# A hybrid encoder layer on one core: the sample's attention first, norms in two stages, block sums under eight fill units

## The chip, the cores and the metric

The kernel runs on one core of one Trainium2 chip. The metric is the device time of one execution in microseconds (us). The kernel before took 868.57 us (median of three executions, 867.28 to 869.51).

## What is computed

The layer treats two sequences with the same weights: a prompt of 512 tokens and a sample of 256. Together they are six blocks of 128 tokens: blocks 0 to 3 are the prompt, 4 and 5 the sample. In the reference, cut to what matters:

```
def mixer(h, ...):
    proj = h @ w_in
    cq, ckv, kr, conv_a, conv_g = jnp.split(proj, cut, axis=-1)
    q = rms_norm(cq, q_norm_g) @ w_uq        # 8 heads, 64 + 32 (rotary)
    kv = rms_norm(ckv, kv_norm_g) @ w_ukv
    ...
    attn = block_attention(qf, kf, v)        # every query sees every key of its sequence
    u = conv_a * jax.nn.sigmoid(conv_g)
    u = depthwise_conv(u, dw_w, width 31) + dw_b
    u = jax.nn.silu(layer_norm(u, conv_ln_g, conv_ln_b))
    merged = jnp.concatenate([rms_norm(attn, attn_out_g), rms_norm(u, conv_out_g)], axis=-1)
    return merged @ w_out

x = x + mixer(rms_norm(x, norm1_g), ...)
x = x + (jax.nn.silu(h @ w_gate) * (h @ w_up)) @ w_down    # h = rms_norm(x, norm2_g)
y = rms_norm(x, final_g)
```

## The kernel before

Matmul operands are split into two fp32r parts (`split`: a cast on ACT, L107 or L110, and a subtraction on DVE, L108 or L111), and a product is three matmuls, high with high, high with low and low with high. All PE matmuls of products go through one helper, `mm`, so they share line L286.

The work runs in stages.

1. Input projections (`pc`, `pq`, `pt`). While they run, the depthwise convolution begins on DVE: 31 taps for each of four channel groups of each sequence, one instruction a tap (L250, writing `acc`; 128x512 for the prompt, 128x256 for the sample). `mm` hands out taps in step with the matmuls (`tap_some`, at a `pace`), the prompt's first. `acc_112` to `acc_115` are the prompt's channel groups, `acc_116` to `acc_119` the sample's.
2. Up-projections: keys (`k_up`, `pku`), values (`v_up`, `pv`), queries (`q_up`, `pqu`, one call a block, its output scaled on ACT and rotated on DVE by `rope`).
3. Attention in twelve units. A prompt unit is one head over four blocks, a sample unit two heads over two blocks. Each unit transposes its queries (`st_q`, `ptq`), multiplies by the keys (`st_s`, `pss`), takes the row maximum on DVE (`ngmx`), the exponential on ACT, transposes the result (`st_t`, `ptp`), copies it on ACT (`PT`) and multiplies by the values (`st_v`, `po`). `unit_step(i)` issues the scores of unit i and the values of unit i-1. Before, the prompt's eight units come first, then the sample's four.
4. Between the units the convolution is finished: `conv_ln` transposes `acc` (`pcl`), takes mean and variance on DVE, an inverse root on POOL, and writes `z` on ACT; `conv_act` transposes back (`pca`), applies the swish on ACT and DVE, squares, and sums the squares on PE with a matrix of ones (`prc`); `conv_split` splits it. `attn_norm` transposes the attention output (`pan`), scales it on DVE to `z`, transposes it back (`pcb`) and splits it.
5. Output projection. `out_conv(b, o, ...)` is the convolution's half for block b and half o of the columns (`pe`, 12 matmuls 128x512), `out_attn` the attention's half (`bank<-wr`). Each ends with an addition to the residual on DVE (`xall`, L766).
6. `x1_norm` of each block: squares on ACT, inverse root on POOL, scaling (L902 on DVE, L904 on ACT), transposes (L907) and copies to `raw`.
7. Feed-forward. Gate and up products use a seven-product scheme on 2x2 blocks of the weights and of the normed input: m1 and m2 use parts B11 and B21 of the input alone, p5, p6, p7 and p4 use its block sums T1, T2, T3, T4, and p3 uses B22. `t_sums` makes the sums of one third of the columns: four DVE operations and four splits. There are 22 units f; three fill units (`NFILL = 3`) run m1 and m2 first, kept in SBUF, and the main loop `g_rest(f)` then runs five products for them and all seven for the others. A product is 12 matmuls 128x384.
8. Down products, final norm, output.

A scheduler orders each engine's queue; each engine works its queue in order. The instructions are issued by the program in the order written, but the scheduler may move an instruction ahead of others on its engine. All DMAs named here are issued on SP's queue.

Pools of SBUF are closed and reused: the attention's `qh` and `ql` lie in memory that `rope` used before, so the first cast to `qh` waits for the last of `rope`. T1 and T2 before lie where the attention's normed parts lie (`mT`), so `t_sums` can't write them until `out_attn` has read those.

## Time and profile before

| | |
|---|---|
| median of the runs | 868.57 us (867.28 to 869.51) |
| profiled execution, time | 872.94 us |
| profiled execution, span | 871.2 us |
| PE busy | 824.6 us (95%) |
| DVE busy | 718.0 us (82%) |
| ACT busy | 438.7 us (50%) |
| POOL busy | 79.0 us (9%) |
| mean granted TensorE clock | 0.975 |
| DMA moved | 108.27 MB |

Durations below come from the one profiled execution. PE and PEld overlap: a weight load runs beside the matmul before it. Two things in PE's row cost time: idle time, and time in which the granted clock is below 1.00, since the same matmuls then take longer.

### The profile page before, as it was taken

The numbers are of one execution on the slowest core, as the hardware profiler recorded it, in microseconds if no ns is written. First come the engines' busy times: TensorE is split into PE (matmuls) and PEld (weight loads), VectorE is DVE, ScalarE is ACT, GpSimd is POOL, SyncE is SP. The second block draws the span as 40 slices with busy tenths as digits, with TensorE's granted clock in tenths as the row PEclk, the third lists the DMA queues.
The fourth block names the chain that finished last, engine by engine and source line by source line (L and its number), as shares of the span: only waits on it lengthen the run. The fifth ranks groups of instructions, "written<-read, shape, count | busy, mean of one in ns | idle before, by whom it ended". The sixth has DMA issues, their size and how long they took to land.

```text
span 871.2 us, 12428 instructions
## 1 busy us (share of the span) xinstructions
PE 824.6 (95%) x4381; PEld 735.8 (84%) x4381; DVE 718.0 (82%) x1310; ACT 438.7 (50%) x886; POOL 79.0 (9%) x113
## 2 busy tenths in 40 slices
PE   5999999899998889979999999999999999999996
PEld 4888997866675667769999999999999988888785
DVE  3699989988878745799998787888898778989994
ACT  5623338777778063584343333343433445556743
POOL 1000341000101010100000000000000000003273
PEclk9999999989989969989999999999999999999999
DMA  8722102300001113224433334443434599963343
GB/s 273 277 68 85 43 1 80 140 1 1 1 1 58 40 48 123 96 72 131 145 124 103 125 103 142 139 143 123 159 125 151 165 319 335 309 216 117 110 134 144
DMA packets 46638, 108.27 MB, mean 124 GB/s; under 512 B 4720, under 2 KB 18032, under 8 KB 46576
## 3 DMA queue, kind: packets, MB, share of 16 engines
q1 hardware_dynamic: 46400, 107.09, 36.7%
q8 instruction: 34, 0.56, 0.3%
q10 hardware_dynamic: 144, 0.39, 0.1%
q14 instruction: 28, 0.23, 0.1%
q0 software_dynamic: 32, 0.00, 0.0%
HBM read 88.20 MB, written 19.27 MB: 123 GB/s over the span
## 4 chain that ended last, share of the span: by engine, by line
PE 79%; DVE 10%; ACT 3%; issue 3%; DMA 2%; POOL 1%; POOLq 0%; ACTq 0%
PE bank L286 51%; PE pc L286 7%; PE pe L286 4%; PE pss L286 3%; PE pq L286 3%; PE po L286 2%; PE pt L286 2%; DVE acc L250 2%; PE ptp L695 2%; DVE wr L108 1%; DMA st<-xT 1%; PE pku L286 1%; DVE ra L108 1%; PE prc L286 1%; DVE ra L491 1%
## 5 line engine op out<-in xcount | busy, mean ns | idle before, releaser
L286 PE MATMUL bank<-ra,wr 128*128 128x384 f32 x1056 | 188.0, 336 | 0.0
L286 PEld LDWEIGHTS bank<-ra,wr 128*128 128x128 f32 x1056 | 184.7, 187 | 0.0
L286 PE MATMUL bank<-sa,wr 128*128 128x384 f32 x792 | 145.4, 341 | 4.9 <-DVE wr L108 4.9
L286 PEld LDWEIGHTS bank<-sa,wr 128*128 128x128 f32 x792 | 141.3, 191 | 5.2 <-DVE wr L108 5.2
L286 PE MATMUL bank<-wr,wr 128*128 128x512 f32 x594 | 135.2, 389 | 1.7 <-DVE wr L108 1.7
L250 DVE SCALAR_TENSOR_TENSOR acc<-u,c,acc 128x512 f32<-128x512 f32 (+1 forms) x240 | 133.0, 608 | 0.1
L286 PEld LDWEIGHTS bank<-wr,wr 128*128 128x128 f32 x594 | 111.4, 188 | 25.2 <-DVE wr L108 2.1
L107 ACT CAST wr<-sr 128x512 fp32r<-128x512 f32 (+1 forms) x107 | 65.7, 616 | 84.4 <-PE bank L286 83.0
L107 ACT CAST wr<-vt 128x512 fp32r<-128x512 f32 x88 | 54.6, 621 | 93.3 <-PE bank L286 83.9
L108 DVE TENSOR_TENSOR wr<-sr,wr 128x512 fp32r<-128x512 f32 (+1 forms) x107 | 72.6, 681 | 18.7 <-ACT wr L107 18.6
L1112 POOL TENSOR_SCALAR fme<-fms 128x1 f32<-128x1 f32 x6 | 27.7, 4608 | 440.3 <-ACT vt L1102 440.1
L286 PE MATMUL pc<-ra,sa 128*128 128x256 f32 (+1 forms) x288 | 56.1, 357 | 9.6 <-ACT ra L110 9.6
L286 PEld LDWEIGHTS pc<-ra,sa 128*128 128x128 f32 x288 | 47.0, 200 | 17.7 <-ACT ra L110 10.5
L108 DVE TENSOR_TENSOR wr<-vt,wr 128x512 fp32r<-128x512 f32 x88 | 60.1, 685 | 0.0
L107 ACT CAST wr<-ra 128x384 fp32r<-128x384 f32 x51 | 26.1, 513 | 37.6 <-PE bank L286 21.8
L108 DVE TENSOR_TENSOR wr<-ra,wr 128x384 fp32r<-128x384 f32 x51 | 28.1, 551 | 9.7 <-ACT wr L107 8.7
L286 PE MATMUL pe<-sa,ra 128*128 128x512 f32 x120 | 32.4, 423 | 2.2 <-ACT sa L110 1.2
L286 PE MATMUL bank<-wr,ra 128*128 128x512 f32 x144 | 34.4, 395 | 0.0
L286 PE MATMUL pq<-sa,ra 128*128 128x384 f32 x108 | 33.8, 342 | 0.0
L678 ACT ACTIVATE sa<-pss,ngmx 128x512 f32<-128x512 f32 (+1 forms) x48 | 29.5, 626 | 7.2 <-DVE ngmx L675 7.2
L286 PE MATMUL pss<-ra,qh 96*128 96x512 f32 (+1 forms) x96 | 31.2, 403 | 1.6 <-ACT sa L678 0.9
L675 DVE TENSOR_REDUCE ngmx<-pss 128x1 f32<-128x512 f32 (+1 forms) x40 | 26.8, 684 | 6.3 <-PE pss L286 5.6
(219 smaller groups left out, 1340.7 us busy)
## 6 DMA issues: line engine op xcount, KB each, us to landing
sr<-wgu SPq DMA_DIRECT2D x47, 512.0 KB, 3.8
sr<-wdn SPq DMA_DIRECT2D x34, 512.0 KB, 4.4
sumd<-xall SPq DMA_DIRECT2D x44, 192.0 KB, 1.9
ra<-sumd SPq DMA_DIRECT2D x44, 192.0 KB, 5.0
actd<-xall SPq DMA_DIRECT2D x11, 384.0 KB, 2.3
xall<-actd SPq DMA_DIRECT2D x11, 384.0 KB, 2.9
st<-wconv SPq DMA_DIRECT2D x7, 512.0 KB, 6.3
xr<-xtok SPq DMA_DIRECT2D x6, 512.0 KB, 6.6
```

Of the source, the lines that this page charges most:

```text
L107: ACT.copy(dst_hi, src)
L108: DVE.tensor_sub(dst_lo, src, dst_hi.bitcast(F32))
L250: yield n / 512, lambda j=j: DVE.scalar_tensor_tensor(a, us[:, j : j + n], w(j), a, ALU.mult, ALU.add)
L286: PE.matmul(out, lhsT, rhs, start=start, stop=stop)
L491: DVE.tensor_sub(lo, src, hi.bitcast(F32))
L675: DVE.tensor_reduce(mx, ps.rearrange("p (j n) -> p j n", j=m), AX.X, ALU.max, negate=True)
L678: ACT.activation(P[:, js], ps[:, js], AF.Exp, bias=ngmx[:, b0 + b, h : h + 1], accum_out=asum[:, b0 + b, h : h + 1],)
L695: PE.transpose(pt[:, o : o + 128], P[b][:, j * n + kt * 128 : j * n + (kt + 1) * 128], ident)
L1112: POOL.tensor_scalar(fme[b], fms[:, 2 * b + 1 : 2 * b + 2], 1.0, EPS, ALU.mult, ALU.add)
```

## The change

Five things are moved or made new; nothing in the number of products changes.

- The attention units are reordered: the sample's four first, then the prompt's eight. `q_up(0)` moves ahead of the sample's `k_up`, and the others run 4, 5, 1, 2, 3. The copies of the rotated key are reordered to match. `conv_ln(0)` now stands after unit 4 (`LN0 = 4`, before 6), `attn_norm(4)` and `(5)` after unit 8, and the prompt's four `attn_norm` after the last unit.
- `attn_norm` and `conv_act` are cut into two stages (`attn_norm1` and `2`, `conv_act1` and `2`), with projection parts written between them; from there on PE's transposes and matmuls are pinned to the written order (`pinned`). The `out_conv(4, 0)` and `(5, 0)` move behind them, into the eight-bank stage.
- The attention's half (`mT`) and the convolution's half (`cvT`) get regions of their own, and T1 to T4 are laid so that T1 and T3 lie over the convolution's half.
- The blocks of the output projection and `x1_norm` run 4, 0, 1, 5, 2, 3; the transposes of `x1_norm` become `x1_turn`, written one or two blocks later.
- There are eight fill units. Their m1 and gate value are written to DRAM (`filld`) and loaded again by `g_rest`. `t_sums` makes two splits (T3, T1), and `t_split2` the other two (T2, T4); they are written behind the first fill units, block column 1 ahead of them. For f = 0, p5 and p7 run before p6. The gate weights of five more units are loaded twice.

The core of the diff:

```diff
-LN0 = 6
+LN0 = 4
...
     def mm(out, lhsT, rhs, start, stop):
-        PE.matmul(out, lhsT, rhs, start=start, stop=stop)
+        pinned(PE.matmul(out, lhsT, rhs, start=start, stop=stop))
...
     kr_up(0)
+    q_up(0)
     for p in range(4):
         k_up(p, 1)
...
-    for b in range(NB):
+    for j, b in enumerate((4, 5, 1, 2, 3)):
         q_up(b)
...
-    units = [(0, (h,)) for h in range(H)] + [(1, (2 * p, 2 * p + 1)) for p in range(H // 2)]
+    units = [(1, (2 * p, 2 * p + 1)) for p in range(H // 2)] + [(0, (h,)) for h in range(H)]
...
-    mT = rtiles()
+    mT = mtiles((0, 4096))
+    cvT = mtiles((8192, 6144))
...
         if i == LN0:
             tap_all(0)
+            pace["s"] = 1.0
+            pin[0] = True
             conv_ln(0)
             conv_ln(1)
+            pin[0] = False
...
-            attn_norm(2, mT)
-            attn_norm(3, mT)
-        elif i == LN0 + 5:
+            attn_norm(4)
+            attn_norm(5)
             conv_split(0)
+        elif i == LN0 + 7:
             wc0 = conv_w(0)
...
+    oc(0, 0)
+    oc(1, 0)
     wc1 = conv_w(1)
...
+    pin[0] = True
...
+    attn_norm1(0)
+    attn_norm1(1)
+    oc(2, 0)
+    attn_norm2(0)
+    attn_norm2(1)
+    attn_norm1(2)
+    attn_norm1(3)
+    oc(3, 0)
+    attn_norm2(2)
+    attn_norm2(3)
...
+    oc(0, 1)
     tap_all(1)
+    oc(1, 1)
     conv_ln(4)
     conv_ln(5)
-    attn_norm(4, mT)
-    attn_norm(5, mT)
-    conv_act(1)
+    oc(2, 1)
+    for k in range(4):
+        conv_act1(1, k)
+    oc(3, 1)
+    for k in range(4):
+        conv_act2(1, k)
     conv_split(1)
...
-    T1, T2, T3, T4 = [[blk(ra_, 2 * i + w) for w in range(2)] for i in range(4)]
+    T2, T4, T3, T1 = [[blk(ra_, 2 * i + w) for w in range(2)] for i in range(4)]
...
+        if f < NFILL:
+            nc.sync.dma_start(filld[f], units_g[f])
...
+        if f < NFILL:
+            A = x_pair()
+            nc.sync.dma_start(A, filld[f])
...
-    NFILL = 3
+    NFILL = 8
...
+    both(4)
+    both(0)
+    x1_turn(4)
+    both(1)
+    x1_turn(0)
+    both(5)
+    x1_turn(1)
...
+    for f in range(3):
+        gs_load(f)
+    both(2)
+    split(wx[0], wx[1], gs[0][:, KA])
+    t_sums(1)
+    out_attn(3, 0, wa[0])
+    gw[0] = wx, wpair(gs[0][:, KB])
+    x1_turn(5)
+    x1_turn(2)
+    out_attn(3, 1, wa[1])
+    prep(1)
+    x1_norm(3)
+    behind = {0: lambda: t_sums(2), 1: lambda: t_sums(0), 2: lambda: t_split2(1), 3: lambda: t_split2(2), 4: lambda: t_split2(0)}
     for f in range(NFILL):
...
+        gs_load(f + 3)
+        g_m1(f, gs[f], gw[f][0])
+        prep(f + 2)
+        if f in behind:
+            behind[f]()
+        g_m2(f, gs[f], gw[f][1])
+        if f == 0:
+            x1_turn(3)
+    pin[0] = False
```

Where this moves instructions, at the three places of which the prediction speaks. The line numbers of the changed kernel differ (`mm` is L293 there, `conv_ln`'s transposes L570, L107 and L108 are the same).

PE's queue at the start of the attention, before. `ptq` are query transposes, `pcl` the transposes of `conv_ln`, `pss` scores:

```order
L650 MATMUL ptq_1796<-ident,sa_171_1423 96x128 x4
L563 MATMUL pcl_2245<-ident,acc_112 128x128
L563 MATMUL pcl_2245<-ident,acc_113 128x128
L563 MATMUL pcl_2245<-ident,acc_114 128x128
L563 MATMUL pcl_2262<-ident,acc_112 128x128
L563 MATMUL pcl_2262<-ident,acc_113 128x128
L563 MATMUL pcl_2262<-ident,acc_114 128x128
L563 MATMUL pcl_2245<-ident,acc_115 128x128
L563 MATMUL pcl_2262<-ident,acc_115 128x128
L286 MATMUL pss_1805<-ra_69,qh_1790 128x512 x2
```

The same place on PE in the changed kernel:

```order
L686 MATMUL ptq_1798<-ident,sa_171_1423 96x128 x4
L293 MATMUL pss_1807<-ra_69,qh_1790 128x256 x2
L293 MATMUL pss_1817<-ra_69,qh_1790 128x256 x2
L293 MATMUL pss_1841<-ra_69,qh_1803 128x256 x2
L293 MATMUL pss_1807<-ra_69,ql_1791 128x256
L293 MATMUL pss_1807<-ra_69,qh_1790 128x256 x2
```

The eight `pcl` transposes of blocks 0 and 1 have moved from here to the place behind the fourth sample unit, and the first scores are a sample unit's.

PE's queue from the end of the output projection's convolution half, before: `pan` and `pcb` are the transposes of `attn_norm`, `pca` and `prc` those and the sums of `conv_act`:

```order
L563 MATMUL pcl_3011<-ident,acc_119 128x128
L611 MATMUL pan_3028<-ident,attnT_1773 128x128 x4
L621 MATMUL pcb_3036<-ident,z_3033 128x128 x4
L611 MATMUL pan_3048<-ident,attnT_1773 128x128 x4
L583 MATMUL pca_3069<-ident,z_3009 128x128
L583 MATMUL pca_3069<-ident,z_3026 128x128
L621 MATMUL pcb_3056<-ident,z_3053 128x128 x4
L583 MATMUL pca_3091<-ident,z_3009 128x128
L583 MATMUL pca_3091<-ident,z_3026 128x128
L286 MATMUL prc_3068<-ones,th_3073 128x2 x2
```

The same place on PE in the changed kernel, from the last value products (`po`) on:

```order
L293 MATMUL pe_2818<-sa_387_2738,ra_69 128x512 x11
L642 MATMUL pan_2850<-ident,attnT_1772 128x128 x4
L642 MATMUL pan_2857<-ident,attnT_1772 128x128 x4
L293 MATMUL pe_2864<-sa_387_2738,ra_69 128x512 x12
L656 MATMUL pcb_2884<-ident,z_2855 128x128 x4
L656 MATMUL pcb_2897<-ident,z_2862 128x128 x4
L642 MATMUL pan_2910<-ident,attnT_1772 128x128 x4
L642 MATMUL pan_2917<-ident,attnT_1772 128x128 x4
L293 MATMUL pe_2924<-sa_387_2738,ra_69 128x512 x12
L656 MATMUL pcb_2943<-ident,z_2915 128x128 x4
L656 MATMUL pcb_2956<-ident,z_2922 128x128 x4
L293 MATMUL pe_2969<-sa_397_2837,ra_69 128x512 x12
```

Projection parts of 12 matmuls now stand between the two transposes of a norm, and the norm is that of the prompt's blocks; `pcl` of blocks 4 and 5 comes 24 `pe` matmuls after the last `pcb`, one more part stands between it and `pca`, and one between `pca` and `prc`.

DVE's queue where the block sums are made, before: `b` are the raw blocks, `ra` the sums' parts, L920 to L926 are `t_sums`, L958 is the addition of a fill unit's m2, and `wr` are parts of the fill units' weights:

```order
L108 TENSOR_TENSOR ra_69<-b_3229,ra_69 128x4x128 x2
L922 TENSOR_TENSOR b_3229<-b_3228,b_3229 128x4x128
L926 TENSOR_TENSOR b_3229<-b_3229,b_3230 128x4x128
L958 TENSOR_TENSOR xall<-bank_3162,xall 128x384
L108 TENSOR_TENSOR ra_69<-b_3229,ra_69 128x4x128 x2
L924 SCALAR_TENSOR_TENSOR b_3229<-b_3229,b_3231 128x4x128
L108 TENSOR_TENSOR wr_3217<-sr_3225,wr_3216 128x512
L108 TENSOR_TENSOR wr_3219<-sr_3226,wr_3218 128x512
```

The same place on DVE in the changed kernel (L997 to L1002 are `t_sums`, L1039 is the addition of m2):

```order
L997 TENSOR_TENSOR vt_1418<-b_3227,b_3225 128x512
L1039 TENSOR_TENSOR xall<-bank_3128,xall 128x384
L999 TENSOR_TENSOR b_3225<-b_3224,b_3225 128x4x128
L108 TENSOR_TENSOR ra_69<-vt_1418,ra_69 128x4x128
L1001 SCALAR_TENSOR_TENSOR b_3227<-b_3225,b_3227 128x4x128
L108 TENSOR_TENSOR wr_3215<-sr_3223,wr_3214 128x512
L1002 TENSOR_TENSOR b_3226<-b_3227,b_3226 128x4x128
L108 TENSOR_TENSOR ra_69<-b_3225,ra_69 128x4x128
L108 TENSOR_TENSOR wr_3217<-sr_3223,wr_3216 128x512
```

The splits of the fill units' weights (`wr`), which stood behind most of the block sums, now stand between them, and 16 products wait for no sum where six did.

More of the change, by code (lines that the diff above doesn't have):

```diff
@@ L573, in conv_ln, with conv_act1 @@
         cz[b] = z
-    def conv_act(s):
+    prcs = {}
+    def conv_act1(s, i):
         b0, nb = SB[s]
         n = SEQ[s][1]
-        pr = pst("o" if s == 0 else "s", "prc")
-        for i in range(4):
-            pt = pst("l", "pca")
-            for b in range(nb):
-                PE.transpose(pt[:, b * 128 : (b + 1) * 128], cz[b0 + b][:, i * 128 : (i + 1) * 128], ident)
+        pt = pst("l", "pca")
+        for b in range(nb):
+            pinned(PE.transpose(pt[:, b * 128 : (b + 1) * 128], cz[b0 + b][:, i * 128 : (i + 1) * 128], ident))
+        if s == 0:
@@ L591, in conv_act @@
-            ACT.activation(th[:, :n], d, AF.Square, scale=0.5 * CC ** -0.5)
-            for b in range(nb):
-                mm(
-                    pr[:, 2 * b : 2 * b + 2], th[:, b * 128 : (b + 1) * 128], ones[:, :2],
-                    start=(i == 0 and b == 0), stop=(i == 3 and b == nb - 1),
-                )
+        else:
+            h = slice(i % 2 * 256, i % 2 * 256 + 256)
+            if i == 0:
+                prcs["y"] = tmp.tile([128, 512], F32, tag="th", name=nm("yt"), bufs=3)
+            if i % 2 == 0:
+                prcs["h"] = tmp.tile([128, 512], F32, tag="th", name=nm("th"), bufs=3)
+            yt, th = prcs["y"][:, h], prcs["h"][:, h]
@@ new lines, in conv_act1, with conv_act2 @@
+        g, bb = c[:, C_LG + i : C_LG + i + 1], c[:, C_LB + i : C_LB + i + 1]
+        ACT.activation(yt[:, :n], pt[:, :n], AF.Identity, bias=bb, scale=g)
+        ACT.activation(th[:, :n], yt[:, :n], AF.Tanh, scale=0.5)
+        d = acc_cols(s, i)
+        DVE.scalar_tensor_tensor(d, th[:, :n], 1.0, yt[:, :n], ALU.add, ALU.mult)
+        ACT.activation(th[:, :n], d, AF.Square, scale=0.5 * CC ** -0.5)
+        prcs[s, i] = th
+    def conv_act2(s, i):
+        b0, nb = SB[s]
+        if i == 0:
+            prcs[s] = pst("o", "prc")
+        pr, th = prcs[s], prcs.pop((s, i))
+        for b in range(nb):
+            mm(
+                pr[:, 2 * b : 2 * b + 2], th[:, b * 128 : (b + 1) * 128], ones[:, :2],
+                start=(i == 0 and b == 0), stop=(i == 3 and b == nb - 1),
+            )
+        if i < 3:
+            return
@@ L769, in w, with oc @@
         def w(k):
[L770 to L772 removed]
+            return [t[:, (k % 2) * 512 : (k % 2 + 1) * 512] for t in wc_[k // 2]]
+        out_mm(p, b, cvT, w)
         out_add(p, b, o, rc)
+    def oc(b, o):
+        out_conv(b, o, wc1 if o else wc0, pst("s", "pe"))
     st_q(0)
@@ L1013, in tile_hybrid_layer, with both @@
     wa = [attn_w(o) for o in range(2)]
-    for b in range(3):
+    wx = [wxp.tile([128, 512], F32R, name=f"wx{i}") for i in range(2)]
+    def both(b):
         for o in range(2):
```

159 lines of the change are left out of this document (86 added, 73 removed).

## The prediction

> **What bounds the kernel now.** I read the page first, then the busy time by stage, then PE's waits, then the queues of DVE and ACT where PE waits. The page says that PE is the bound on average:
>
> ```profile
> PE 824.6 (95%) x4381; PEld 735.8 (84%) x4381; DVE 718.0 (82%) x1310; ACT 438.7 (50%) x886; POOL 79.0 (9%) x113
> ```
>
> So only PE's idle time and its time at a lower clock can be won. By stage (the columns are the stretch, its length, then busy time with instructions of PE, PEld, DVE, ACT and POOL, then the granted clock):
>
> ```profile
> 137.00:176.25 39.25, 32.84 (x191) 30.03 (x189) 38.77 (x78) 30.96 (x68) 0.00 (x0) 0.99 0.24 93
> 176.25:279.50 103.25, 97.86 (x537) 68.40 (x537) 85.71 (x176) 78.51 (x192) 9.51 (x22) 0.92 0.01 3
> 279.50:323.70 44.20, 37.35 (x162) 30.27 (x161) 27.09 (x56) 16.33 (x35) 4.54 (x12) 0.85 0.16 55
> 323.70:396.90 73.20, 63.91 (x306) 54.24 (x305) 55.66 (x89) 41.15 (x84) 5.71 (x12) 0.95 0.30 101
> 396.90:820.00 423.10, 423.10 (x2272) 403.21 (x2272) 362.91 (x649) 187.30 (x343) 9.18 (x3) 1.00 0.50 168
> ```
>
> These are: end of the up-projections; attention; projection of the convolution's half with the last norms; projection of the attention's half, block sums, fill units and the first block-sum product; the rest. Loss is idle time plus busy time times one less the clock: 6.4 in the first; 5.4 + 0.08 x 97.9 = 13.2 in the second; 6.9 + 0.15 x 37.4 = 12.5 in the third; 9.3 + 0.05 x 63.9 = 12.5 in the fourth; none in the fifth. Together 44.6 us, the most that could be won; the change leaves the start and the end alone. PE's waits between 137 and 400 us (total, times, longest):
>
> ```profile
> PE bank L286 <- DVE wr L108: 4.9, 1, 4.9
> PE pan L611 <- ACT z L572: 3.6, 1, 3.6
> PE bank L907 <- DVE vt L902: 3.2, 5, 0.7
> PE pcl L563 <- DVE acc L250: 2.9, 1, 2.9
> PE po L286 <- ACT PT L697: 2.3, 1, 2.3
> PE pku L286 <- DVE ck L108: 1.7, 1, 1.7
> ```
>
> Five of these six names are places that the change rewrites; the reader is to ask of each what ends last there once it is gone.
>
> **First stretch, 137 to 176 us: nothing.** Moving `q_up(0)` ahead of the sample's `k_up` gives PE 18 matmuls to run while DVE makes `ck`, so the wait of 1.7 goes. Moving `pcl` away takes the wait of 2.9 out. But DVE was busy 38.77 of the 39.25 us, and ACT's first cast to `qh` shows who ends last:
>
> ```profile
> 175.62 1.07 ACT L107 CAST qh<-ptq 96x512 fp32r<-96x512 f32 x2 [5.18 <-DVE sa L371]
> ```
>
> It waits 5.18 us for the last `rope`, which stands at the end of DVE's backlog (the same 120 prompt taps and 5 sample taps, splits and ropes in both kernels). PE comes there earlier and waits longer; scores start at about 176.3 as before. The price: the eight `pcl` transposes that ran in this shadow must run later, in PE's busy time.
>
> **Second stretch, attention.** Where its loss of 13.2 lies, with that of later places:
>
> ```profile
> 176.25:186.00 9.75, 9.75 (x35) 7.68 (x36) 7.16 (x13) 5.57 (x15) 0.00 (x0) 0.69 0.00 0
> 250.00:265.00 15.00, 13.88 (x76) 11.97 (x76) 8.22 (x16) 8.95 (x25) 3.08 (x6) 0.66 0.00 1
> 265.00:280.00 15.00, 11.29 (x73) 7.52 (x74) 14.87 (x31) 14.93 (x40) 1.74 (x4) 1.00 0.09 26
> 300.00:305.00 5.00, 1.08 (x8) 0.60 (x6) 2.02 (x6) 1.55 (x2) 1.98 (x6) 1.00 0.00 0
> 305.00:315.00 10.00, 8.08 (x29) 6.30 (x30) 3.60 (x7) 6.03 (x15) 1.49 (x4) 0.51 0.16 52
> 383.00:395.00 12.00, 7.31 (x26) 7.31 (x27) 11.22 (x20) 7.21 (x12) 0.00 (x0) 0.72 0.37 105
> ```
>
> The start costs 0.31 x 9.75 = 3.0 in clock, after the idle time before it. 250 to 265 costs 1.1 + 0.34 x 13.9 = 5.8: short sample units mixed with `prc` and transposes. 265 to 280 costs 3.7, with ACT busy 14.93 of 15: exponentials, casts of `conv_split`, squares and `conv_w` at once. The change puts the short units where nothing else is to be done, and the convolution's work among the prompt's long units, where the stretch as a whole has ACT busy 78.5 of 103. So the 5.8 and 3.7 should shrink. Not to nothing: `conv_ln` now takes four groups of transposes through two banks in two units, each through a chain of 4.5 us (below), and the sample units at the start are short chains at a half clock. The trace doesn't show that mix. The loss besides the start was 10.2; bounds are 0 and 12 (a fifth more, if the chains wait); I take 6, just past the middle, since ACT stays the nearest limit. Rates of PE:
>
> ```profile
> 279.51 20.04 PE L286 MATMUL pe<-sa,ra 128*128 128x512 f32 x87
> 299.39 1.03 PE L563 MATMUL pcl<-ident,acc 128*128 128x128 f32 x8
> ```
>
> A 512-wide matmul takes 20.04 / 87 = 0.23, eight transposes 1.0. Work at full rate before: 103.25 - 13.2 = 90.05. Added: 8 `pcl`, 1.0. Taken out to the next stretch: 16 transposes of the prompt's norms, 2.0, and 6 of 9 `pe`, 1.4. That leaves 87.65. With 3.0 at the start and 6 besides, attention ends at 176.25 + 96.65 = 272.9, where it ended at 279.5.
>
> **Third stretch: DVE's queue sets it.** Prices on DVE, by rows in which the next instruction follows at once (start to start, the last 0.08 of each overlapping), and the row maximum from the page:
>
> ```profile
> 276.11 2.73 DVE L111 SCALAR_TENSOR_TENSOR sa<-st,c,sa 128x512 fp32r<-128x512 f32 x4
> ...
> 284.16 2.06 DVE L250 SCALAR_TENSOR_TENSOR acc<-u,c,acc 128x256 f32<-128x256 f32 x5
> 286.14 0.74 DVE L766 SCALAR_TENSOR_TENSOR xall<-pe,rc,xall 128x512 f32<-128x512 f32 x1
> ...
> 379.27 1.28 DVE L108 TENSOR_TENSOR ra<-b,ra 128x512 fp32r<-128x512 f32 x2
> ```
>
> ```profile
> L675 DVE TENSOR_REDUCE ngmx<-pss 128x1 f32<-128x512 f32 (+1 forms) x40 | 26.8, 684 | 6.3 <-PE pss L286 5.6
> ```
>
> So a tap 0.40, a scaled split 0.66, a residual addition 0.66, other 512-wide operations 0.60. After the last scores PE has 27 `ptp`, 8 `po` and 3 `pe` left of the attention, 3.4 + 1.8 + 0.7 = 5.9; the last `ngmx` ends 0.7 after those scores, at 272.9 - 5.9 + 0.7 = 267.7. Behind it the new order has, up to the last tap, 43 taps (34 before), 8 scaled splits, 5 additions, 4 `z` products and 4 splits: 17.2 + 5.3 + 3.3 + 4.8 = 30.6, so 298.3. PE alone would be there at 272.9 + 69 x 0.23 + 4.0 = 292.8. DVE is late by 5.5: about 2.6 at the first `pcb` (its `z` stands behind 23 taps and the 8 splits), 0.8 at the second, the rest at `pcl`. Then `conv_ln` and `conv_act` of the sample:
>
> ```profile
> 300.26 1.28 DVE L566 BATCH_NORM_STATS2 bst<-pcl 128x6 f32<-128x512 f32 x2
> ```
>
> ```profile
> 303.21 1.66 ACT L572 ACTIVATE z<-pcl,nmr,r 128x512 f32<-128x512 f32 x2 [21.80 <-POOL nmr L570]
> ```
>
> ```profile
> 314.03 0.55 ACT L587 ACTIVATE yt<-pca,c 128x256 f32<-128x256 f32 x1
> 314.62 0.42 ACT L591 ACTIVATE th<-acc 128x256 f32<-128x256 f32 x1
> ```
>
> From the end of `pcl` (300.42) to the second `z` (304.87) are 4.45; 12 `pe` (2.7) stand beside it. ACT then has four rounds of `yt`, tanh, square and cast, 0.59 + 3 x 0.32 = 1.55 each, 6.2 in all, beside 8 `pca` and 12 `pe`. So: 298.3 + 1.0 + 4.45 + 0.3 + 6.2 = 310.3. Before, 323.7 stood behind 24 more `pe`, now moved: 5.5. Equal point 315.8, 7.9 earlier.
>
> **Fourth stretch.** Before, `t_sums` for three columns, 24 operations of 0.60 = 14.4 on DVE, stood ahead of fill splits (`wr`), and PE waited 4.9 and then ran at 0.72: 4.7 + 0.28 x 7.3 = 6.8 there. Now 16 products stand ahead, 16 x 2.1 = 33.6 us of PE, and DVE has beside them 16 splits, 8 additions and about 18 of the 24 operations: 9.6 + 3.8 + 10.8 = 24.2. The sums are hidden. The five waits at L907 go where cover is longer than the chain:
>
> ```profile
> 349.69 0.76 DVE xall L766
> ...
> 352.88 1.22 PE bank L907 x8
> ```
>
> 3.2 us from the end of a block's projection to its transposes; two blocks (24 matmuls, 5.5) or one and a half now stand between. Block 3's chain has casts of fill weights in ACT's queue ahead of it, about 5 against 4.2 of cover. I leave 2.5 of 12.5 (bounds 0 and 6), so 10.0 is won. In the main loop the eight filled units keep DVE nearly full:
>
> ```profile
> 396.92 0.56 DVE L977 TENSOR_TENSOR xall<-bank,xall 128x384 f32<-128x384 f32 x1 [0.26 <-PE bank L286]
> ...
> 407.00 0.55 DVE L977 TENSOR_TENSOR xall<-bank,xall 128x384 f32<-128x384 f32 x1
> ```
>
> A filled unit takes 10.1 (10.5 for 60 matmuls at the fill's rate); DVE needs 9 x 0.60 + 9 x 0.47 = 9.6 of it. Three such units ran without a PE wait; eight should. The extra DMA (five weight loads, eight stores, eight loads) lies on queues busy 0.50 of the time.
>
> **Sum.** 0 + 7.9 + 10.0 = 17.9, so the profiled execution, 872.94, goes to 855.0. The median before is 4.4 below that execution; I take the gain off the median: **850.7**. Its own range: 846 to 856 (attention's loss 2 to 11).
>
> **Rivals.**
> *Attention gives nothing* (0.20): the loss besides the start stays at 10 and the chains wait 4 more, since `pcl` and `pca` share two banks and ACT's queue. For it: the 5.8 of 250 to 265 came with little idle time, so its cause is not ACT alone. Only the fourth stretch pays: 858.6.
> *Dense* (0.13): no loss but the start's, and the fourth stretch whole: 6 + 2.5 more, 842.
> *The clock falls* (0.12). After the wait of 3.6 at `pan` PE ran 305 to 315 at 0.51 and lost 4.0; after one of 2.3 and a shorter one, 265 to 280 stayed at 1.00. If DVE's 5.5 fall together at `pcl`, 4 more are lost: 855. The Trainium skill, "TensorE: Matmul & The Clock Gate", section "What's actually happening", says that an idle window of about 3.4 us halves the clock. By that rule my split waits cost nothing and a joined one does; these two rows agree, while 250 to 265 at 0.66, with 1.1 idle in all, doesn't follow from it.
> *Slower* (0.04): m1 comes back from DRAM too late.
>
> ```profile
> xall<-actd SPq DMA_DIRECT2D x11, 384.0 KB, 2.9
> ```
>
> SP's queue is in order, and a reload stands behind weight loads that wait for DVE. A late one holds p6's addition, and DVE's queue behind it. Each us counts eight times; from 2.6 a unit the kernel is slower, at 3 it is 850.7 + 24 = 875. Against: the landing takes 2.9, and the slot is free two units, 20 us, ahead.
> *No change* (0.04): the four sample units, at a half clock with little beside them, wait 4.5 us each: 868.6. Against: sample units before waited 3.7 in 15 us with ACT full.
>
> Forecast 0.47. Range 842 to 861: outside lie slower, no change, and about 0.1 at the ends of dense and of the first rival. A difference of 0.3% is about what can be told from none: faster 0.92, same 0.04, slower 0.04.
>
> **What would show it.** Scores still start near 176, after a longer wait on `qh`. ACT has no full 15 us. Last tap near 298, `pcb` waiting for `z`; the wait on `wr` gone; main loop without PE idle. Wrong if DVE's taps end past 305, or if a wait on reloaded `xall` shows.

## The result and the profile after

The changed kernel takes 846.52 us (median of four executions, 843.55 to 850.85) where the kernel before takes 868.83 beside it: ratio 0.975, interval 0.970 to 0.980. A second set, later, gave a median of 847.08 (five executions, 843.94 to 849.91). In that set and in two others single executions ran longer as a whole (856.63 there, 913.88 with `e2_back`, 923.99 with the kernel before); medians and ranges here leave them out. The profiled execution took 845.79 us, with a span of 844.0.

The page of the profile after, its row of engines:

```profile
PE 810.1 (96%) x4381; PEld 722.9 (86%) x4381; DVE 714.8 (85%) x1310; ACT 434.4 (51%) x886; POOL 87.9 (10%) x113
```

PE's instructions are as many as before, and its busy time is 14.5 us less: the same matmuls ran at a higher granted clock. The other part of the gain is idle time, 46.6 before and 33.9 now. Busy time by stretch, with the columns as in the prediction (length; PE, PEld, DVE, ACT, POOL; clock). The work in them isn't quite that of the rows of before: 137 is an earlier point of the work there, attention has 13 fewer of PE's instructions, the third lacks the 24 `pe` that moved behind 302, and the fourth ends with the last transposes of the block norms:

```profile
137.00:173.75 36.75, 28.77 (x168) 26.56 (x166) 35.68 (x73) 27.59 (x62) 0.00 (x0) 0.96 0.23 87
173.75:266.60 92.85, 90.63 (x524) 61.91 (x524) 81.49 (x167) 77.20 (x187) 8.51 (x18) 0.98 0.04 12
266.60:302.00 35.40, 31.00 (x158) 24.52 (x158) 28.07 (x60) 13.79 (x34) 5.80 (x14) 0.98 0.14 45
302.00:362.00 60.00, 57.84 (x272) 48.26 (x273) 41.95 (x67) 32.98 (x70) 8.30 (x14) 0.95 0.32 108
362.00:820.00 458.00, 456.68 (x2442) 431.70 (x2440) 403.10 (x724) 209.89 (x392) 33.86 (x6) 1.00 0.55 183
```

From 137 us to the end of the fourth, PE is idle for 16.8 us; before it was 27.9 up to 396.9. PE's largest waits in that part (1.0 at `ptq` and 0.9 at `prc` are left out):

```profile
PE pss L293 <- ACT qh L107: 5.3, 1, 5.3
PE bank L982 <- ACT vt L973: 2.2, 2, 1.7
PE pqu L293 <- DVE ra L498: 1.7, 2, 1.1
PE pca L590 <- ACT z L579: 1.3, 2, 0.8
PE pcb L656 <- DVE z L644: 1.2, 2, 0.7
PE pcl L570 <- DVE acc L250: 0.8, 1, 0.8
```

Of the six waits shown before, four are gone (`wr` 4.9, `pan` 3.6, `po` 2.3, `pku` 1.7) and two are shorter; the largest that is left, on `qh`, is new in this size, and that of the query products on `ra` (1.7) is new.

**The half-clock stretches.** The granted clock has two values, 1.00 and 0.50. Cut into fine windows, the trace of before shows five stretches at half clock behind 137 us, each with both edges inside 0.1 us:

```profile
175.50:182.33 6.83, 6.20 (x17) 4.82 (x17) 4.46 (x9) 3.36 (x9) 0.00 (x0) 0.51 0.00 0
254.01:264.25 10.24, 10.24 (x49) 8.74 (x49) 4.35 (x9) 5.18 (x16) 3.08 (x6) 0.50 0.01 2
305.21:315.45 10.24, 8.53 (x32) 6.62 (x32) 3.46 (x8) 6.37 (x15) 1.49 (x4) 0.50 0.15 51
318.86:322.27 3.41, 3.41 (x11) 2.83 (x10) 1.20 (x4) 2.42 (x5) 1.07 (x2) 0.51 0.02 5
387.13:393.95 6.82, 6.26 (x20) 6.26 (x21) 6.39 (x11) 4.19 (x8) 0.00 (x0) 0.50 0.53 157
```

After, there are two there, the second after a window in which PE was busy for 2.86 of 3.42 us:

```profile
171.13:177.96 6.83, 4.19 (x19) 4.16 (x20) 5.75 (x13) 1.07 (x2) 0.00 (x0) 0.50 0.00 0
297.42:300.84 3.42, 2.86 (x19) 2.45 (x17) 2.21 (x6) 3.42 (x11) 0.00 (x0) 1.00 0.00 0
300.84:307.66 6.82, 6.49 (x17) 5.31 (x18) 3.70 (x9) 5.48 (x10) 1.59 (x2) 0.50 0.36 108
```

PE was busy for 34.6 us at half clock before and for 10.7 after; half of that is lost, 17.3 and 5.3. So the change won about 12 us of clock and 11 of waiting. Every stretch is a multiple of 3.41 us long, and the starts of before's five lie 23, 15, 4 and 20 times 3.41 apart: the clock is set on a fixed grid of windows. The prediction counted this loss (as part of its 44.6 us) but put it down to waits and short units.

**Where the 27.2 us between the two profiles lie.** The equal points are the first `k` product, the first score, the end of `po` and the sample's projection. Before, the group of `k` products (its last numbers are the first and the last start), and PE's timeline:

```profile
L286 PE MATMUL pku<-ck,w x48: 278/386/475, 130.3 to 147.5; 128*128 128x512 f32 x24, 128*128 128x256 f32 x24
```

```profile
323.66 5.60 PE L286 MATMUL bank<-sa,ra 128*128 128x512 f32 x24
```

After, the same two views:

```profile
L293 PE MATMUL pku<-ck,w x48: 278/335/475, 127.0 to 146.2; 128*128 128x512 f32 x24, 128*128 128x256 f32 x24
```

```profile
173.77 1.65 PE L293 MATMUL pss<-ra,qh 96*128 96x256 f32 x6 [5.31 <-ACT qh L107]
...
263.84 2.79 PE L293 MATMUL po<-PT,vt 128*64 128x512 f32 x10
...
288.89 1.86 PE L570 MATMUL pcl<-ident,acc 128*128 128x128 f32 x8 [0.83 <-DVE acc L250]
...
302.04 13.82 PE L293 MATMUL bank<-sa,ra 128*128 128x512 f32 x48
```

The start, up to `pku`, gave 3.3: the first input landed earlier in this execution, which the change doesn't touch. From `pku` to the first score: 45.95 before, 46.75 after, a loss of 0.8. Attention: 103.25 to 92.85, 10.4 won, of which 2.4, by the prediction's count, is work that moved to the next stretch. From there to the sample's projections, with the 24 moved `pe` (5.6) added after: 44.2 to 41.0, 3.2 won. From there to the end: 547.5 to 536.4, 11.1 won, of which about 2.7 is the speed of the main loop in these two executions (below). Without the 3.3 and the 2.7 the change is worth 21.2 in this profile; the medians say 22.3.

A profile of a later execution of the same kernel, the one that took 847.19, has the same first and third stretch, and its main loop has the same speed. But its attention took 95.8 us, from 172.59 to the `pe` that follow this row:

```profile
265.68 2.79 PE L293 MATMUL po<-PT,vt 128*64 128x512 f32 x10
```

So attention won 7.4 there, not 10.4, because a stretch at half clock lay in the prompt's `prc` (shown in experiments 10 to 12).

### The profile page after: what moved, and what is told of

The parts are those of the page before. It is cut to its first block, busy times and chain, and to the rows that moved or that the text cites. A ratio compares the mean times of both kernels' runs of the same rounds, so it can differ in the third digit from the quotient of the medians.

```text
span 844.0 us, 12490 instructions
## 1 busy us (share of the span) xinstructions
PE 810.1 (96%) x4381; PEld 722.9 (86%) x4381; DVE 714.8 (85%) x1310; ACT 434.4 (51%) x886; POOL 87.9 (10%) x113
## 4 chain that ended last, share of the span: by engine, by line
PE 54%; DVE 4%; issue 3%; DMA 1%; POOL 1%; ACT 1%; POOLq 0%; ACTq 0%; DVEq 0%
PE bank L293 53%; DVE wr L108 1%; DMA sr<-wdn 1%; DVE sr L1308 1%; DVE ra L108 1%; DVE xall L1214 0%; DVE sa L108 0%; DVE xall L1227 0%; PE bank L982 0%; POOL nmv L969 0%; POOL fmv L1241 0%; POOL fmr L1242 0%; DVE vt L1218 0%; POOL nmr L971 0%; ACT vt L1226 0%
## 5 line engine op out<-in xcount | busy, mean ns | idle before, releaser
L293 PE MATMUL bank<-ra,wr 128*128 128x384 f32 x1056 | 186.6, 335 | 0.0
L293 PEld LDWEIGHTS bank<-ra,wr 128*128 128x128 f32 x1056 | 183.4, 188 | 0.0
L293 PE MATMUL bank<-sa,wr 128*128 128x384 f32 x780 | 139.2, 335 | 0.0
L293 PE MATMUL bank<-wr,wr 128*128 128x512 f32 x594 | 135.1, 389 | 1.3 <-DVE wr L108 1.3
L293 PEld LDWEIGHTS bank<-sa,wr 128*128 128x128 f32 x780 | 135.5, 188 | 0.0
L293 PEld LDWEIGHTS bank<-wr,wr 128*128 128x128 f32 x594 | 111.4, 188 | 24.8 <-DVE wr L108 1.7
L107 ACT CAST wr<-vt 128x512 fp32r<-128x512 f32 x88 | 54.6, 620 | 97.7 <-PE bank L293 92.6
L107 ACT CAST wr<-sr 128x512 fp32r<-128x512 f32 x106 | 64.7, 616 | 61.3 <-PE bank L293 60.0
L108 DVE TENSOR_TENSOR wr<-sr,wr 128x512 fp32r<-128x512 f32 x106 | 71.9, 683 | 14.7 <-ACT wr L107 14.7
L1236 POOL TENSOR_SCALAR fme<-fms 128x1 f32<-128x1 f32 x6 | 33.9, 5644 | 418.3 <-ACT vt L1226 418.0
L293 PE MATMUL pc<-ra,sa 128*128 128x256 f32 (+1 forms) x288 | 54.4, 350 | 8.2 <-ACT ra L110 8.2
L108 DVE TENSOR_TENSOR wr<-vt,wr 128x512 fp32r<-128x512 f32 x88 | 60.1, 685 | 0.0
L293 PEld LDWEIGHTS pc<-ra,sa 128*128 128x128 f32 x288 | 45.8, 195 | 15.8 <-ACT ra L110 8.6
L107 ACT CAST wr<-ra 128x384 fp32r<-128x384 f32 x51 | 26.0, 512 | 33.1 <-PE bank L293 21.2
L293 PE MATMUL pss<-ra,qh 96*128 96x512 f32 (+1 forms) x96 | 30.4, 397 | 6.2 <-ACT qh L107 5.3
L108 DVE TENSOR_TENSOR wr<-ra,wr 128x384 fp32r<-128x384 f32 x51 | 28.1, 551 | 8.5 <-ACT wr L107 8.3
L293 PE MATMUL bank<-wr,ra 128*128 128x512 f32 x144 | 34.2, 394 | 0.0
L293 PE MATMUL pq<-sa,ra 128*128 128x384 f32 x108 | 33.8, 342 | 0.0
L293 PEld LDWEIGHTS bank<-wr,ra 128*128 128x128 f32 x144 | 26.7, 188 | 5.6
L293 PE MATMUL bank<-sa,ra 128*128 128x512 f32 x114 | 30.3, 419 | 0.1
```

The lines of the kernel that those rows point to most:

```text
L107: ACT.copy(dst_hi, src)
L108: DVE.tensor_sub(dst_lo, src, dst_hi.bitcast(F32))
L293: pinned(PE.matmul(out, lhsT, rhs, start=start, stop=stop))
L1236: POOL.tensor_scalar(fme[b], fms[:, 2 * b + 1 : 2 * b + 2], 1.0, EPS, ALU.mult, ALU.add)
```

## The experiments

**1 and 2. The two halves alone.** `e1_front` is the new order up to the sample's projection of the convolution's half, with the old feed-forward part; `e2_back` is the reverse.

```diff
 e1_front: new code up to out_conv(5, 1), then
+    both halves of blocks 0..5 in order, t_sums(0..2), NFILL = 3, nothing pinned
 e2_back: old code up to out_conv(5, 1), with mT and cvT in regions of their own, then
+    blocks 4 0 1 5 2 3, sums behind eight fill units
```

> The new order up to the sample's last projection of the convolution's half, and behind it the old feed-forward part (blocks 0 to 5 in order, block sums ahead of three fill units, nothing kept in DRAM). Theory (the two halves are worth what they are worth alone): at equal points of the two profiles the front gained 12.7 us and the back 11.1, so this kernel keeps about 12 of the gain: 868.8 - 12 = 857, between 854 and 860, with the wait on the fill weights (4.9 before) and the clock fall behind it back. Rival (the back's gain hangs on the front, since the block order 4 first needs the sample's norms early): the back's gain is lost wholly and more, 860 to 864, or the front brings nearly all, 848 to 851.

> The old order up to the sample's last projection of the convolution's half, and behind it the new feed-forward part (blocks 4 0 1 5 2 3, sums spread over eight fill units kept in DRAM). Theory (additive): 868.8 - 11 = 858, between 855 and 861; the half-clock stretches at 175, 254, 305 and 319 us stay, the one at 387 goes. Rival (the back needs the front's early norms of the sample): less than 5 us gained, 864 to 869.

Measured: e1_front 860.99 (ratio 0.992, interval 0.988 to 0.995), e2_back 856.66 (three executions, 855.32 to 858.60; 0.987, 0.983 to 0.990), both against 869.35. That is 8.4 and 12.7 us; together 21.0, within the errors of the 22.3 of both. So the halves add, as far as errors of about 3 us each can tell. e1_front by itself lies 1 us outside the theory's range and in the rival's; what decides is e2_back, which has its 12.7 us without the sample's early norms. In e2_back's profile the stretch at 387 is gone, as expected; four others are there, at 172.3, 247.4, 267.8 and 302.0, and none where before had its short one at 319. e1_front has the old wait back, by PE's waits (5.0 of the 6.1; the other 1.2 is at 818 us), and a stretch at half clock behind it, by a window:

```profile
PE bank L293 <- DVE wr L108: 6.1, 2, 5.0
```

```profile
374.70:381.50 6.80, 5.74 (x19) 5.74 (x20) 6.80 (x12) 4.55 (x9) 0.00 (x0) 0.54 0.46 154
```

**3. The sums ahead of the fill units**, with the transposes of block 3, the one change being their place:

```diff
+    x1_turn(3)
+    t_sums(2); t_sums(0); t_split2(1); t_split2(2); t_split2(0)
     for f in range(NFILL):
...
-        if f in behind: behind[f]()
-        if f == 0: x1_turn(3)
```

> The changed kernel with only the block sums moved back: all sums and their splits stand ahead of the eight fill units, with the transposes of block 3. Theory (hidden behind the fill units, the sums cost nothing; ahead of them DVE has 18 operations of 0.60 = 10.8 us between the last splits that were made in advance and the next ones): PE waits 3 to 6 us for split fill weights and falls to half clock for at least one stretch of 3.4 us behind it: 6 to 9 us slower than the changed kernel, 852 to 856. Rival (it was the block order that hid the chains, and the first two units, split in advance, cover the sums anyway): within 2 us of the changed kernel, 845 to 849.

Measured 855.06 (853.49 to 857.86), 8.5 slower than the changed kernel, as expected in size, but not for the reason given. PE did not wait for split weights there; it waited for the block that I had moved along, by its waits and the window behind them:

```profile
PE bank L982 <- ACT vt L973: 6.5, 2, 4.8
```

```profile
360.90:367.70 6.80, 5.64 (x21) 5.64 (x22) 6.40 (x11) 5.80 (x11) 0.35 (x1) 0.51 0.08 31
```

From the sample's projection to the end the profile is 6.8 us longer than that of the changed kernel. The waits at these transposes grew by 4.3 (6.5 where there were 2.2), and half of 5.6 at half clock is 2.8; together 7.1. Another 1.8 came earlier, from a longer stretch at half clock at the first scores (13.7 us long), which the edit doesn't touch. What this shows is the price of `x1_turn` without its cover, not that of the sums.

**4. Three fill units instead of eight**, with the same sums behind them, separates the two:

```diff
-    NFILL = 8
+    NFILL = 3
-    behind = {..., 2: lambda: t_split2(1), 3: lambda: t_split2(2), 4: lambda: t_split2(0)}
+    behind = {..., 2: lambda: [t_split2(k) for k in (1, 2, 0)]}
```

> The changed kernel with three fill units instead of eight (the three kept in DRAM as before); the same sums stand behind the three. Theory (cover: three units give PE 6 x 2.1 = 12.6 us, DVE has 18 operations of 0.60 and 1.7 us a unit, 16 us, so PE waits 3 to 4 us at the first products that read the sums, perhaps with a fall to half clock): 3 to 7 us slower than the changed kernel, 849.5 to 853.5. Rival (the sums are no longer what PE waits for, the order of blocks was the gain): 845 to 848.

Measured 858.43 (852.38 to 862.36), slower than the changed kernel by more than expected. By PE's timeline it waits three times at the first products that read the sums, twice for parts of the sums (`ra`) and once for a split weight (`wr`), and a stretch at half clock follows (374.1 to 381.0):

```profile
372.39 0.44 PE L293 MATMUL bank<-ra,wr 128*128 128x384 f32 x1 [1.40 <-ACT ra L107]
374.15 0.69 PE L293 MATMUL bank<-ra,wr 128*128 128x384 f32 x1 [1.32 <-DVE ra L108]
375.87 9.43 PE L293 MATMUL bank<-ra,wr 128*128 128x384 f32 x39 [1.03 <-ACT wr L107]
```

3.8 of waits and half of 5.8 busy at half clock are 6.7. The four executions spread over 10 us; the profiled one, 861.13, had the slowest speed of the main loop (48 products in 8.64, see 7), which makes some 6 us more. The waits and the stretch, which the changed kernel has not, show that three units are too few and that eight are cover for the sums; how much of the 11.9 between the medians is due to that, the runs don't separate.

**5. Fewer taps.** The result lacks them; the other work is the same.

```diff
-        for j in range(1, KW):
+        for j in range(1, KW - (3, 5)[s]):
```

> The changed kernel without the last 3 prompt taps and the last 5 sample taps of each channel group: 12 prompt taps of 0.60 and 20 sample taps of 0.40 us are left out of DVE's queue and of the result. Theory (DVE's queue sets both the first scores and the last tap): the wait of 5.3 us for the first cast of q falls by 4 or more, the last tap ends some 8 us earlier against the attention's end, the waits of PE for the norms behind it (0.7, 0.6, 0.8) go, and the tail from the last tap to the sample's projection, 12.2 us, stays but has less to hide: in all 7 to 10 us faster than the changed kernel, 836 to 840. Rival (ACT's and POOL's short chains set these places, DVE is merely busy): the waits stay and the time is within 2 us of 846.

Measured 841.02 (840.29 to 844.06), 5.5 faster; expected were 7 to 10. Half of the theory held. In the third stretch PE no longer waits at `pcb` and `pcl`, and from the end of the last `po` (268.3) to the sample's projection are 30.2 us, where the changed kernel has 35.4; 1.2 of this is five `pe` products that now ran before that end. Counted from `pku`, the projection starts 3.2 earlier; behind it the stretch at half clock is 3.4 us long and not 6.8, and 1.9 more are won. PE's timeline, at `pcl`:

```profile
286.44 1.03 PE L570 MATMUL pcl<-ident,acc 128*128 128x128 f32 x8
```

At the first score nothing moved: the wait on `qh` stayed at 5.3, since the pace put sample taps where the prompt's had been, and DVE was as full as before, 6.00 of the 6.00 us before the first cast (the window's third busy time):

```profile
167.00:173.00 6.00, 1.06 (x8) 0.81 (x8) 6.00 (x19) 0.30 (x1) 0.00 (x0) 0.94 0.00 0
```

That DVE's backlog sets this wait fits that row, but no run here took the backlog away.

**6. The same by other engines.** 11 of the sample's taps go to ACT (the product) and GpSimd (the addition), nothing left out:

```diff
+            if s == 1 and i == 3 and j >= 20:
...
+                ACT.activation(t, us[:, j : j + n], AF.Copy, scale=w(j))
+                POOL.tensor_tensor(a, a, t, op=ALU.add)
```

> The changed kernel with 11 of the sample's taps (channel group 3, taps 20 to 30) taken off DVE: ACT makes the product, GpSimd adds it to the accumulator. Theory (DVE's queue sets the last tap; without 20 sample taps the stretch from the attention's end to the sample's projection was 30.2 us where the changed kernel has 35.4): 11 x 0.40 = 4.4 us less for DVE, the waits for the norms' z (0.7, 0.6) and the last tap (0.8) go: 2 to 4 us faster, 842.5 to 844.5. Rival (GpSimd's adds, for which no row exists, are slow or slow DVE down, so that group 3 becomes the late one): slower, 849 or more.

Measured 842.67 (840.79 to 850.94), ratio 0.972 (0.966 to 0.978): in the expected range, but its interval overlaps that of the changed kernel. In the profile PE no longer waits for a tap, and from the last `po` to the sample's projection are 32.75 us, 2.7 fewer than in the changed kernel. The additions took 0.92 each and nobody on PE waited for them; their group in the profile:

```profile
L256 POOL TENSOR_TENSOR acc<-acc,tp 128x256 f32<-128x256 f32 x11 | 10.2, 923 | 27.9 <-PE pss L303 18.5 <-ACT tp L255 9.4
```

(The 18.5 is GpSimd's own idle time ahead of the first.) DVE as the setter of the third stretch now stands on two runs.

**7. The sample's sums of squares elsewhere.**

```diff
-    for k in range(4):
-        conv_act2(1, k)
     conv_split(1)
...
+    out_mm of block 4, both halves; then conv_sq(1, k) and conv_act2(1, k) for k in range(4)
```

> The changed kernel with the sample's eight 2-column sums of squares (prc) taken from the place between its last convolution work and its first projection to behind that block's two products, and its squares on ACT behind the splits. Theory (the clock is set by how much of the window before PE spent moving columns; a 2-column product occupies PE but counts as hardly any work): the window 297 to 301 us, in which PE stood under prc and its waits, now holds projections, the half-clock stretch of 6.8 us that began at 300.8 is gone (3.3 us) and PE goes from the last pe to the first sample product with 1 us of wait where it lost 3.2: 4 to 6 us faster than the changed kernel, 840.5 to 842.5. Rival (the clock falls after idle time alone, and the splits set the start of the projection anyway): the fall stays, at most 1.5 us gained, 845 to 847.

Measured 847.67 (846.21 to 848.73): no gain in time, so a miss, though in the profile all that was expected of the place came about. The stretch at half clock is gone and the sample's projection starts earlier, with two short waits; PE's timeline and a window at the place:

```profile
298.54 0.73 PE L293 MATMUL bank<-sa,ra 128*128 128x512 f32 x2 [0.49 <-ACT ra L107]
299.73 5.29 PE L293 MATMUL bank<-sa,ra 128*128 128x512 f32 x22 [0.46 <-DVE ra L108]
304.86 1.84 PE L293 MATMUL bank<-ones,th 128*128 128x2 f32 x16
```

```profile
302.00:306.00 4.00, 4.00 (x26) 3.49 (x24) 0.00 (x0) 0.10 (x1) 0.00 (x0) 1.00 0.00 0
```

Counted from `pku`, the first attention product comes at 186.0 us where the changed kernel had 188.7. What took it back in this execution is the main loop, whose products ran slower throughout: 48 of them in 8.64 us, where the profile of the changed kernel has 8.48. One group of each timeline, first of c1_prc:

```profile
429.47 8.64 PE L293 MATMUL bank<-ra,wr 128*128 128x384 f32 x48
```

Of the changed kernel:

```profile
421.26 8.48 PE L293 MATMUL bank<-ra,wr 128*128 128x384 f32 x48
```

Of the kernel before:

```profile
427.63 8.55 PE L286 MATMUL bank<-ra,wr 128*128 128x384 f32 x48
```

The page of the changed kernel has 1056 + 780 such matmuls, 38 groups of 48; 0.16 more for each is 6.1 us. For the other three executions this account need not hold: their mean granted clock is 0.988 to 0.990, where the profiled one has 0.995, which is up to 4 to 6 us more lost at half clock, and there is no profile to say where. So why the median shows no gain stays open.

**8. Is idle time needed for the clock to fall?** In the main loop PE has no gap. Four trains of 2-column products are added there, 64, 32, 16 and 8 in a row.

```diff
+        for _ in range({12: 64, 14: 32, 16: 16, 18: 8}.get(f, 0)):
...
+            PE.matmul(tr[:, 0:2], ident, ones[:, :2], start=True, stop=True)
```

> The changed kernel with four trains of 2-column products added to units of the main loop, where PE otherwise has no gap and full clock: 64, 32, 16 and 8 in a row (about 7.7, 3.8, 1.9 and 1.0 us at 0.12 each). Theory (the clock follows the share of a fixed window of 3.41 us in which columns move): the train of 64 fills at least one whole window and the clock falls to half with no idle time; 32 do so in most positions; 8 never. Rival (only idle time lowers the clock, as PE's busy time shows it): the clock stays at 1.00 through all four. In both the time grows by the trains, about 14 us less what DVE's queue hides nothing of: 858 to 866.

One execution, 899.65 us, where 858 to 866 was expected. The row count is doubled, two matmul rows for each product. Rows of the four trains, then windows of the first (its first 2.8 us, then the rest) and of the last:

```profile
548.73 24.70 PE L1167 MATMUL bank<-ones,ident 128*128 128x2 f32 x128
...
605.26 9.69 PE L1167 MATMUL bank<-ones,ident 128*128 128x2 f32 x64
...
646.84 3.63 PE L1167 MATMUL bank<-ones,ident 128*128 128x2 f32 x32
...
681.30 1.84 PE L1167 MATMUL bank<-ones,ident 128*128 128x2 f32 x16
```

```profile
548.73:551.55 2.82, 2.82 (x27) 2.82 (x27) 2.82 (x6) 1.14 (x2) 0.00 (x0) 1.00 0.08 33
551.55:573.30 21.75, 21.75 (x105) 21.75 (x104) 1.22 (x3) 0.00 (x0) 0.00 (x0) 0.50 0.05 19
681.30:683.00 1.70, 1.70 (x17) 1.70 (x17) 1.70 (x4) 1.14 (x2) 0.00 (x0) 1.00 0.19 77
```

PE is busy without a gap, and the clock falls to half 2.8 us into the first train; it comes back 5.4 us behind its end (at 578.85). The second train brought a stretch of 10.2 us, the third one of 3.4, the last none. The theory is shown and its rival refuted: 2-column products keep PE busy in its row, but not its clock up. The size was off: a product took 0.23 at full clock, not 0.12, and about 0.4 at half clock, so the trains together took 39.9 us and not 14.

The same trace shows that the speed of the main loop can change within an execution. It had 8.54 or 8.55 for 48 products ahead of the trains, 8.64 between the second and the third, 8.55 behind the third and 8.64 behind the last, all at full clock. Two of these groups:

```profile
506.81 8.54 PE L293 MATMUL bank<-ra,wr 128*128 128x384 f32 x48
...
634.12 8.64 PE L293 MATMUL bank<-ra,wr 128*128 128x384 f32 x48
```

**9. The stretch at 254 us of the kernel before.** 12 of the prompt's 16 sums of squares are left out, so the prompt's convolution norm is another.

```diff
             for b in range(nb):
+                if s == 0 and i:
+                    continue
...
                 mm(pr[:, 2 * b : 2 * b + 2], th[...], ones[:, :2], ...)
```

> The kernel before with 12 of the prompt's 16 2-column sums of squares left out (only the first channel group's stay, so the prompt's convolution norm is not the reference's). Theory (these products under the sample's short units made the windows at 250.6 to 260.8 too empty of moving columns): the half-clock stretch of 10.2 us from 253.9 on is gone or down to one window, 4 to 6 us with the 1 to 2 us of the products themselves: 5 to 7 us faster than before, 862 to 864. Rival (the short units with their waits lower the clock by themselves): the stretch stays, 866 to 868.

Measured 863.73 (ten executions, 862.23 to 867.14), ratio 0.995 (0.993 to 0.997): 4.6 us faster than before. The clock stays at 1.00 through the whole place, with the sample's short units and their waits still there:

```profile
245.00:262.00 17.00, 14.24 (x108) 11.12 (x108) 16.24 (x31) 16.80 (x50) 5.04 (x10) 1.00 0.00 1
```

Attention took 97.3 us in this profile, where that of before has 103.3. Some 2.8 of these 6.0 are the 12 products themselves (0.23 each at full clock, by experiment 8). That the stretch is absent only because the grid lay otherwise is not excluded by one profile; against it, e2_back's profile, with the old order and another place of the grid, has a stretch of the same 10.24 us here (247.4 to 257.6). So the largest stretch that the new order removed from attention came from `prc` standing among short units. In the new order it stands among the prompt's long ones, and there it can still bring a stretch, as the next runs show.

**10 to 12. The changed kernel again, and two versions made from the above.** `v1` is experiments 6 and 7 together; `v2` adds six products of 512 columns that nobody reads, into the wait for `qh`.

> The changed kernel once more, beside the next two on the same chip. In the profiles so far the main loop runs at one of three speeds for a whole execution (48 products of 384 columns in 8.48, 8.54 or 8.64 us), whatever the kernel; 1.9% of the 420 us of that loop is 8 us. Theory (this is what spreads the executions of one kernel from 843.6 to 850.9): times again between 843 and 852, median 844 to 849. Rival (the first set was lucky as a whole): median above 850.

> The changed kernel with both: the 2-column products behind the first sample products, and 11 taps on ACT and GpSimd. By the profiles, the place where the first attention product starts, counted from the first k product, came 2.7 us earlier by the one and 2.0 by the other (with 1.6 lost to a longer half-clock stretch at the first scores in that execution). Theory (they act at different waits, so they add): 4 to 6 us faster than the changed kernel on the same chip, 839 to 844. Rival (both only move the same chain behind the last tap, or the main loop gives it back, as the time of the first alone, 847.7, suggests): within 2 us of the changed kernel.

> The combined kernel and, in the 5.3 us in which PE waits for the first cast of q, six products of 512 columns whose result nobody reads (identity times the last block's q, ready when that block's projection is copied). Theory (a window with moving columns keeps the clock, whatever they are for): no half-clock stretch at the first scores, which in the profiles of this front cost 2.1 to 5 us; the first score itself not more than 0.5 us later: 2 to 5 us faster than the combined kernel (844.7), 839.5 to 843, and 4 to 7 faster than the changed kernel. Rival (the fall there comes from the work behind it, short units on a busy DVE and ACT, or the added products only push the scores back): 844 to 848, the stretch at half clock stays.

On one chip the changed kernel had 847.08 (843.94 to 849.91, besides the one at 856.63, which lies outside the expected range; ratio 0.975, 0.972 to 0.978) and v1 844.75 (840.11 to 848.16; 0.973, 0.969 to 0.976), just outside its range. v1 is the lower by 2.3, but the intervals overlap, so that it beats the changed kernel isn't shown. That the main loop spreads the executions isn't shown either, and for the first set the record speaks against it: its slowest, 850.85, had a mean granted clock of 0.982 and its fastest, 843.55, one of 0.991; 0.009 of 845 us is 7.6, and 7.3 lie between them. From `pku` to the first attention product v1 has 186.6 us, the two profiles of the changed kernel 188.7 and 191.7. The second of these has a stretch at half clock in the prompt's `prc` that the first has not, with the same order and the same waits. Of the eleven profiles with the new order of attention, two have one there, this one and, 3.4 us long, that of v2. By a window of the second:

```profile
224.60:231.40 6.80, 6.80 (x24) 4.47 (x24) 4.39 (x10) 3.12 (x7) 1.71 (x2) 0.53 0.00 0
```

v2 took 851.68, slower than v1: a miss. Its products did keep the clock at the first scores, and the fall came one place later, since the second unit's `ptq` had moved behind them and PE then waited 2.0 for `ql`. Three windows, of the added products, of that wait, and of the stretch:

```profile
171.00:177.80 6.80, 6.32 (x30) 3.82 (x28) 6.77 (x18) 1.60 (x4) 0.00 (x0) 1.00 0.00 0
178.00:181.20 3.20, 0.84 (x5) 0.64 (x5) 3.20 (x8) 0.96 (x4) 0.00 (x0) 0.96 0.00 0
181.20:188.00 6.80, 6.68 (x30) 5.68 (x30) 4.66 (x10) 5.13 (x20) 0.00 (x0) 0.52 0.01 2
```

The rest of its loss fits a main loop at 8.64 in its profile. All six executions have a mean granted clock of 0.988 to 0.993, no lower than those of v1, so it isn't time at half clock that makes them slow; what does stays open.

## Why the prediction was right, step by step

The forecast, 850.7, was 4.2 above the measured median; the range and the sign held, and so did the places from which the gain was to come. The gain came to 22.3 where 17.9 was predicted. By steps the first profile has -0.8, 10.4, 3.2 and 8.4, together 21.2; the second has -0.8, 7.4, 3.2 and 8.9, together 18.7. Of the signs, the last tap came at 289.9 and not near 298, and no 15 us have ACT full, though 222 to 237 has it busy for 14.4; the others held.

- *First stretch, 0.* Measured a loss of 0.8. The waits on `pku` and `pcl` went and PE waited 5.3 on `qh` instead, as the step said, and 1.7 at the query products, which it had not.
- *Attention, 6.6 won.* Measured 10.4, and 7.4 in the second profile. The term that was mis-sized is the loss besides the start: 6 taken, between bounds of 0 and 12; what was left in the first profile is 1.5 (PE was busy for 88.53 of the 90 us from 180 on, all at full clock). The "dense" rival had this term right there; in the second profile a stretch of 6.8 us at half clock comes on top, and the 6 taken is near the 4.5 lost. Which of the two an execution gets, no step foresaw, so that 6.6 is near the second is luck. The step took the 5.8 lost at 250 to 265 for a matter of short units under a full ACT; it was 10.24 us at half clock, and experiment 9 shows that `prc` brought it. I had let that loss shrink with the load on ACT; it either goes or, where `prc` and waits fill a window again, comes back by whole windows.
- *Third stretch, 1.3 won of its own.* Measured 3.2. DVE's queue as the limit held (experiments 5 and 6): 32.0 us from the last `ngmx` to the last tap where 30.6 was worked out, and 12.1 from there to the sample's projection where 12.0 was. But PE had 8.6 us of attention left behind the last `ngmx`, not 5.2: behind the last scores stood 16 `po`, the values of two units, where the step counted 8. PE alone would have been at the last tap at 266.6 + 69 x 0.23 + 4.0 = 286.5, so DVE, at 289.9, was late by 3.4 and not by 5.5. That the clock would hold because the waits are split was wrong: it fell at 300.8, behind `prc`.
- *Fourth stretch, 10.0 won.* Measured about 8.4 without the main loop's speed. The sums are hidden (no wait on them is left, and with three units it is back, experiment 4). The loss is 5.1 where 2.5 was left for it: 2.2 of waits at the transposes, near that, and 2.9 in the stretch at half clock carried in from the third, for which the step had no term.
- *Main loop, 0.* From 362 to 820 us PE is idle for 1.3, at one wait in the down products (at 799.7); no wait on a reloaded `xall` shows, so the "slower" rival has nothing for it here.
- *The clock as a rival.* It was made to hang on one wait joined at `pcl`. The Trainium skill, "TensorE: Matmul & The Clock Gate", section "What's actually happening", says that the clock falls after an idle window of about 3.4 us and that this window is free-running and doesn't restart with a kernel. The grid agrees with every stretch here. That the window must be idle doesn't: the clock fell behind a window busy for 2.86 of 3.42 us, and in experiment 8 with no idle time at all.

## What to carry to other kernels

Where PE looks busy and is slow, cut the granted clock into windows of 3.4 us and look at what PE did in the window before each fall: products of a few columns and small waits together empty a window as a long wait does. Put such products behind work that is ready, where none of the three profiles that have them there (c1_prc, v1, v2) shows a fall; among long ones two of eleven still did. Price a stretch at half clock as half of PE's busy time in it. When an engine that is busy without a gap sets the end of a stage, two rows tell how late it will be: what is queued behind its last release, and how much work the other engine still has then; the second was the one that I got most wrong.
